# A hybrid attention block on one core: tiles at new address places, and one weight split ordered behind a product

## The chip, the core and the metric

The kernel runs on one core of a Trainium2 chip. The metric is device time in microseconds for one execution, and the time of a kernel is the median over its runs. The engines are named as the profile names them: PE is TensorE (matrix products), DVE is VectorE, ACT is ScalarE, POOL is GpSimd, and SP is SyncE, whose queue issues most of the DMA transfers.

## What is computed

One decoder block on 512 tokens of width 2048, in fp32. The normed input goes through one input projection. Half of the width feeds eight heads of sparse attention (width 128, two key groups: scores over compressed blocks, selected blocks and a window, mixed by gates); the other half feeds sixteen heads of sliding-window attention with sinks (width 64). Each head's result is multiplied by a SiLU of a gate projection, then comes the output projection, the residual and a final RMSNorm.

```python
h = _rmsnorm(x, norm_g[l])
proj = h @ w_in[l]
(qa, kca, vca, ksa, vsa, kwa, vwa, za, ga, qb, kb, vb, zb) = jnp.split(proj, offsets, axis=-1)
...
o_a = gates[..., 0:1] * o_cmp + gates[..., 1:2] * o_sel + gates[..., 2:3] * o_win
y_a = o_a.reshape(B, S, WIDTH_A) * jax.nn.silu(za)
...
y_b = o_b.reshape(B, S, WIDTH_B) * jax.nn.silu(zb)
x = x + jnp.concatenate([y_a, y_b], axis=-1) @ w_out[l]
return _rmsnorm(x, final_g)
```

## The kernel before

**Products.** Every fp32 operand is split into a high and a low word of the type fp32r: ACT copies (rounds) the high word, DVE subtracts it to get the low word (`split`, L541 to 544; `load_unit`, L88). `mm3` (L118 to 121) then issues three matmuls for one product: weights high with high, low with high, high with low. Most matmuls have 128x128 weights (the stationary operand) and 256 or 512 moving columns.

**Places.** A words tile is 1088 fp32 words long per partition, and 1024 of them are used. The argument of `words(place)` (L80) says at which word the used part begins: MOVING 0, EVEN 16, STILL 32, BELOW 48, so at 0, 64, 128 or 192 bytes into the tile. A word is 4 bytes, and the tile's length is a multiple of 256 bytes, so a place is the same modulo 256 bytes in every buffer of this kind. x's words `xh` and `xl` have tiles of their own (L108, L109), and later the heads' results `yh`, `yl` (L1001) are read back into the same memory for the output projection.

**Stages**, by the trace's clock: up to 45 us the sums for the norm and the first 512-column projections; 45 to 291 the sixteen sliding-window heads, interleaved with 512-column projections; 291 to 353 the compress stage, in which `tok_chunk` (x's words as weights, words of wv1 or wv0 moving) alternates with `compress_unit` (tokens' words as weights, words of cw1 moving); 353 to 425 keys and the first gated projections; 425 to 665 the eight sparse heads; 648 to 679 the last units of wo0 (the first part of the output projection); from 679 the rest of the output projection, built of products of summed blocks.

**Heads.** `pair(h)` (L669) makes one head's queries and gate by `seven(2 + h)` (L574), a scheme of seven block products named 22, p, 21, 12, u, w, q instead of eight, in which the weights are stationary (at STILL) and tokens' words move. `x1` to `x4` are the quarters of the weights, loaded by SP into the tiles `raw`, and `unit` (L546) splits them into whi and wlo. At the end of `pair` DVE multiplies the gate by the inverse root: `last["jj"]`, L677, printed as zr<-zr,rstdb; then ACT takes a tanh of it (L681, printed as st<-zr) and DVE finishes the SiLU (L682). The queries are rotated (POOL adds t<-t,t, L664) and split: qh on ACT (L260), ql on POOL (L261) for the heads 0 to 5. `attn_a` (L908) then does the scores (L932: sp<-KH,qh, sp<-KL,qh, sp<-KH,ql), the exponentials, transposes of the weights (tp) and the products with the values (op). `finish` (L270) multiplies op into the gated result st, which SP writes to memory as yd (L272). The heads 4 to 7 use the second key group, so KH and KL are loaded again (L1027) between head 3 and head 4.

**What sets the order.** Each engine works through its instructions in one order. The program's text gives dependencies, and a list planner places the instructions on the engines by them; `tc.issue_after(a)` adds the demand that what follows stands behind `a`. From about 426 us on this order changes wherever the dependencies or the buffers change.

## Time and profile before

| | us |
|---|---|
| median of three runs | 802.01 |
| the profiled execution's own time | 802.8 |
| its span, first to last instruction | 801.0 |
| PE busy | 789.6 (99%) |
| DVE busy | 686.3 (86%) |
| ACT busy | 504.7 (63%) |
| POOL busy | 108.3 (14%) |

Busy shares are averages over the whole span; how one stage is limited is read from the rows of that stage. In a timeline the first column is when an instruction starts, the second how long it takes; two matmuls overlap, so that the pace of PE is the difference between the starts of neighbours and not the duration. An idle time stands in brackets with what ended it.

### The profile page before, as it was taken

The page shows a single profiled execution, that of the slowest core. Times are in us where ns is not written, and L with a number is a line of the kernel's source. Part 1 is how long each engine was busy: PE and PEld are TensorE (multiplying, and loading weights), DVE is VectorE, ACT ScalarE, POOL GpSimd, SP SyncE. Part 2 cuts the span into 40 slices and gives each one's busy share as a digit, 9 for nine tenths or more (in the row PEclk, how much of TensorE's full clock was granted, in tenths as well). Part 3 has the DMA queues.
Part 4 walks back from the last instruction along what each step waited for, and adds up shares of the span by engine and source line. Part 5 has one row for each costly group of instructions (what it writes and reads, how often), then busy time and mean ns, then how long its engine had stood idle before and what let it go on. Part 6 is the DMA issues. An engine that isn't in the chain of part 4 may idle for free.

```text
span 801.0 us, 15316 instructions
## 1 busy us (share of the span) xinstructions
PE 789.6 (99%) x5693; PEld 739.1 (92%) x5693; DVE 686.3 (86%) x1407; ACT 504.7 (63%) x1103; POOL 108.3 (14%) x111
## 2 busy tenths in 40 slices
PE   9999999999999999999999999999999999999996
PEld 8788888888888899999999999999999999999996
DVE  7668988889989597759999999998999798978895
ACT  6646657655666356664447778777777867553545
POOL 3615002110121000323210110110100000000000
PEclk9999999999999999999999999999999999999998
DMA  7572243564373469887723213225216836797845
GB/s 239 172 242 81 79 144 106 171 171 150 101 210 106 158 200 281 257 269 194 207 82 106 68 53 119 82 92 159 71 50 216 296 120 219 257 266 193 258 86 211
DMA packets 49563, 131.05 MB, mean 164 GB/s; under 512 B 6000, under 2 KB 8848, under 8 KB 49488
## 3 DMA queue, kind: packets, MB, share of 16 engines
q1 hardware_dynamic: 43376, 110.89, 42.3%
q0 software_dynamic: 5824, 18.65, 10.5%
q8 instruction: 45, 0.74, 0.4%
q10 hardware_dynamic: 288, 0.52, 0.2%
q14 instruction: 30, 0.25, 0.1%
HBM read 113.23 MB, written 16.81 MB: 162 GB/s over the span
## 4 chain that ended last, share of the span: by engine, by line
PE 86%; DVE 6%; DMA 3%; ACT 2%; issue 2%; POOL 0%; SPq 0%; DVEq 0%; ACTq 0%
PE pj L119 16%; PE pj L121 15%; PE pj L120 15%; PE oa L120 5%; PE oa L119 5%; PE oa L121 5%; PE sp L932 4%; PE bank L121 2%; PE bank L120 2%; PE bank L119 2%; DMA xr<-xT 2%; DVE wlo L543 2%; PE tp L969 2%; PE tp L384 2%; DMA raw<-wq 1%
## 5 line engine op out<-in xcount | busy, mean ns | idle before, releaser
L119 PE MATMUL pj<-xh,whi 128*128 128x256 f32 (+1 forms) x592 | 196.9, 333 | 0.6 <-ACT t L608 0.5
L121 PE MATMUL pj<-xh,wlo 128*128 128x256 f32 (+1 forms) x592 | 196.2, 331 | 0.0
L120 PE MATMUL pj<-xl,whi 128*128 128x256 f32 (+1 forms) x592 | 196.1, 331 | 0.0
L119 PEld LDWEIGHTS pj<-xh,whi 128*128 128x128 f32 x592 | 111.4, 188 | 11.0 <-ACT t L608 0.9
L121 PEld LDWEIGHTS pj<-xh,wlo 128*128 128x128 f32 x592 | 111.4, 188 | 10.1
L120 PEld LDWEIGHTS pj<-xl,whi 128*128 128x128 f32 x592 | 111.4, 188 | 9.7
L543 DVE TENSOR_TENSOR wlo<-raw,whi 128x1024 fp32r<-128x1024 f32 (+2 forms) x80 | 92.9, 1172 | 7.8 <-ACT whi L542 7.2
L542 ACT ACTIVATE whi<-raw 128x1024 fp32r<-128x1024 f32 (+2 forms) x80 | 77.6, 985 | 30.7 <-DVE raw L581 11.5
L99 DVE TENSOR_TENSOR wlo<-raw,whi 128x1024 fp32r<-128x1024 f32 (+1 forms) x61 | 72.1, 1184 | 22.8 <-ACT whi L97 22.3
L97 ACT ACTIVATE whi<-raw 128x1024 fp32r<-128x1024 f32 (+1 forms) x60 | 56.6, 945 | 28.8 <-PE pj L120 14.8
L120 PE MATMUL oa<-wlo,xh 128*128 128x256 f32 x200 | 55.5, 278 | 0.0
L119 PE MATMUL oa<-whi,xh 128*128 128x256 f32 x200 | 55.4, 278 | 0.0
L121 PE MATMUL oa<-whi,xl 128*128 128x256 f32 x200 | 55.2, 276 | 0.0
L121 PE MATMUL pj<-pu,wlo 128*128 128x256 f32 x160 | 45.0, 281 | 0.5 <-DVE wlo L543 0.5
L119 PE MATMUL pj<-pu,whi 128*128 128x256 f32 x160 | 45.1, 282 | 0.4 <-DVE zr L581 0.4
L120 PE MATMUL pj<-pu,whi 128*128 128x256 f32 x160 | 44.7, 279 | 0.0
L289 DVE TENSOR_TENSOR pl<-tp,ph 128x512 fp32r<-128x512 f32 (+1 forms) x64 | 40.7, 651 | 3.1 <-ACT ph L288 2.9
L288 ACT ACTIVATE ph<-tp 128x512 fp32r<-128x512 f32 (+1 forms) x64 | 34.1, 560 | 9.6 <-PE tp L969 4.4
L363 ACT ACTIVATE ttb<-ttb,sums 128x256 f32<-128x256 f32 (+1 forms) x64 | 30.0, 471 | 14.4 <-DVE sums L356 14.4
L121 PEld LDWEIGHTS oa<-whi,xl 128*128 128x128 f32 x200 | 37.6, 188 | 0.0
L120 PEld LDWEIGHTS oa<-wlo,xh 128*128 128x128 f32 x200 | 37.6, 188 | 0.0
L119 PEld LDWEIGHTS oa<-whi,xh 128*128 128x128 f32 x200 | 37.5, 188 | 0.0
(401 smaller groups left out, 2369.8 us busy)
## 6 DMA issues: line engine op xcount, KB each, us to landing
raw<-wq SPq DMA_DIRECT2D x41, 512.0 KB, 4.4
raw<-wz SPq DMA_DIRECT2D x36, 512.0 KB, 4.0
cw<-cw SPq DMA_DIRECT2D x32, 256.0 KB, 4.0
raw<-wos SPq DMA_DIRECT2D x14, 512.0 KB, 5.9
rw<-wos SPq DMA_DIRECT2D x10, 512.0 KB, 4.8
xr<-xT SPq DMA_DIRECT2D x16, 256.0 KB, 3.4
rows<-xT SPq DMA_DIRECT2D x8, 512.0 KB, 4.7
raw<-wo SPq DMA_DIRECT2D x8, 512.0 KB, 6.0
```

The source lines that it names most:

```text
L97: last["hi"] = act.activation(hi[:, :width], rw[:, :width], AF.Copy).ins
L99: last["lo"] = dve.tensor_tensor(out=lo[:, :width], in0=rw[:, :width], in1=hi[:, :width].bitcast(F32), op=ALU.subtract).ins
L119: pe.matmul(ps, ah, bh, start=first, stop=False, skip_group_check=go_on)
L120: pe.matmul(ps, ah, bl, start=False, stop=False, skip_group_check=go_on)
L121: recent["mm"] = pe.matmul(ps, al, bh, start=False, stop=last, skip_group_check=go_on).ins
L288: act.activation(ph, tp, AF.Copy)
L289: dve.tensor_tensor(out=pl, in0=tp, in1=ph.bitcast(F32), op=ALU.subtract)
L363: act.activation(tv, tv, AF.Exp, bias=mn[:, e, v:v + 1], scale=-1.0, accum_out=dn[:, e, v:v + 1])
L384: pe.transpose(tp[:, o:o + P], tts[kt + s][:, v, c0:c0 + P], ident)
L542: split_hi = act.activation(hi, src, AF.Copy).ins
L543: last["lo"] = dve.tensor_tensor(out=lo, in0=src, in1=hi.bitcast(F32), op=ALU.subtract).ins
L932: pe.matmul(sp[:, a:b], qq[:, qs], kk[:, ko:ko + b - a], start=pi == 0, stop=pi == 2)
```

## The change

Most of it moves tiles. BELOW goes away: `compress_unit`'s words now begin at MOVING like those of `tok_chunk`. The words of wo0 and of the output projection's products (`halves`, `pair`) move from MOVING to EVEN, 64 bytes further. `yh` and `yl` begin 16 words (64 bytes) further in the memory of x's words, which are now one tile `slabs`; so a result that is read back can overlap two neighbouring rows of x's words. Small tiles get longer, `space` tiles are put in as pads, `vbf` takes a buffer of the tag `ob`, and the row flag moves from the tile gt to the tile small, with a small transfer of its own. The single matmul `step` ahead of the output projection gets other addresses. In the built program, counted modulo 256 bytes, a moving tile at MOVING starts at 128, at EVEN at 192, x's words at 192, and y's words at 192 before and 0 after.

One edit is about order: in head 1 (`seven(3)`, i == 3) the split of the quarter x3, which product 21 uses, is put behind `last["jj"]`, the multiply of head 0's gate by the inverse root.

```diff
 CMP = 32
-MOVING, EVEN, STILL, BELOW = 0, 16, 32, 48
+MOVING, EVEN, STILL = 0, 16, 32
 WARM = 40
...
     const = ctx.enter_context(sb("const"))
+    gt = const.tile([P, KT], F32, name="gt")
     wp = ctx.enter_context(sb("wp", bufs=3))
...
     bmask = tab[:, 512 + NQ * CMP:768 + NQ * CMP]
-    small = const.tile([P, 8], F32, name="small")
+    small = const.tile([P, 16], F32, name="small")
     rstd, eps = small[:, 0:NQ], small[:, NQ:NQ + 1]
...
     gates = const.tile([P, NQ, 24], F32, name="gates")
-    gt = const.tile([P, KT + 1], F32, name="gt")
-    rowvalid = gt[:, KT:KT + 1]
+    rowvalid = small[:, 8:9]
 
...
     xpool = ctx.enter_context(sb("xpool", side="right"))
-    xh = xpool.tile([P, KT, S], F32R, name="xh")
-    xl = xpool.tile([P, KT, S], F32R, name="xl")
+    slabs = xpool.tile([P, 2 * KT * S + 64], F32R, name="x")
+    xh, xl = [slabs[:, e * KT * S:(e + 1) * KT * S].rearrange("p (k s) -> p k s", s=S) for e in range(2)]
     angles = xstack.enter_context(sb("angles", side="right"))
...
 
-    flat = xh.rearrange("p k s -> p (k s)")
+    flat = slabs[:, 0:KT * S]
 
...
         if k == 0:
-            nc.sync.dma_start(gt, gT)
+            nc.sync.dma_start(gt, gT[:, 0:KT])
         nc.sync.dma_start(xr, xT[:, k, :])
...
         nc.sync.dma_start(tab, tabs)
+        nc.sync.dma_start(rowvalid, gT[:, KT:KT + 1])
     dve.tensor_tensor(out=cosB, in0=cosB, in1=rstdb, op=ALU.mult)
...
 
-    vbf = wb.tile([P, NQ, P], F32, name="vbf")
+    vbf = wb.tile([P, NQ, P], F32, name="vbf", tag="ob")
+    KBH = wb.tile([P, 2, S], F32R, name="KBH")
+    KBL = wb.tile([P, 2, S], F32R, name="KBL")
     sk = wb.tile([P, 5, 16], F32, name="sk")
...
     act.activation(sk[:, 1, :], sk[:, 0, :], AF.Copy, scale=-1.0)
-    KBH = wb.tile([P, 2, S], F32R, name="KBH")
-    KBL = wb.tile([P, 2, S], F32R, name="KBL")
     VB = wb.tile([P, NQ, 2, P], F32R, name="VB")
...
         for part in range(2):
-            sums = wk.tile([P, 3, 2, 2], F32, name="sums", tag="sums")
+            sums = wk.tile([P, 6, 2, 2], F32, name="sums", tag="sums")
             mn, dn, ex = sums[:, 0], sums[:, 1], sums[:, 2]
...
     VC = [kv.tile([P, P], F32R, name=f"VC{g}") for g in range(2)]
+    kv.tile([P, 48], F32, name="space")
     ahead = ExitStack()
...
         if not final:
-            u2 = unit(x3)
+            with tc.issue_after(last["jj"]) if i == 3 else nullcontext():
+                u2 = unit(x3)
             prod(pb[:, H0], u2, "21", False)
...
     early, ready = quarters[:1], quarters[1:]
-    places = [words(MOVING), words(BELOW), words(BELOW)]
+    places = [words(MOVING) for n in range(3)]
 
...
             cacc[1] = bank(4)
-        compress_unit(1, u, cacc[1], words(BELOW))
+        compress_unit(1, u, cacc[1], words(MOVING))
         if 1 <= u <= 3:
...
     KH, KL = [kv.tile([P, CMP + 1056], F32R, name=f"K{e}")[:, 0:CMP + 1024] for e in "HL"]
+    kv.tile([P, 16], F32, name="space")
     for e, k in enumerate((KH, KL)):
...
             tt = wa.tile([P, 1792 if pair else 768], F32, name=f"tt{pair}", tag=f"tt{pair}")
-            sums = wk.tile([P, 2, 2, 3], F32, name="sums", tag="sums")
+            sums = wk.tile([P, 4, 2, 3], F32, name="sums", tag="sums")
             mn, dn = sums[:, 0], sums[:, 1]
...
 
-    yh, yl = [[w[:, (2 * f + 1) % 17, :] for f in range(16)] for w in (xh, xl)]
+    yh, yl = [[slabs[:, (e * KT + (2 * f + 1) % 17) * S + 16:][:, 0:S] for f in range(16)] for e in range(2)]
 
...
                      (1, 3, (7,))):
-        hi, lo = load_unit(wo0[:, c, u], 1024, place=MOVING, loaded=first_units.pop(0) if first_units else None, after=last["qh"],
+        hi, lo = load_unit(wo0[:, c, u], 1024, place=EVEN, loaded=first_units.pop(0) if first_units else None, after=last["qh"],
                            after_lo=low_y[11] if (c, u) == (0, 2) else last["turn"])
...
                 combos(m)
+    cmb.tile([P, 48], F32, name="space3")
     banks1 = banks(1)
-    step(banks1[3], flat[:, 3 * S - 16:3 * S + 112], flat[:, 2 * S + 32:2 * S + 288])
+    step(banks1[3], flat[:, 2 * S:2 * S + P], flat[:, 3 * S - 16:3 * S + 240])
     for T in range(2):
...
     def halves(raw, to=None):
-        hi, lo = to or words(MOVING)
+        hi, lo = to or words(EVEN)
         split_to(hi, lo, raw)
...
             def pair():
-                return words(MOVING)
+                return words(EVEN)
 
...
                 act.activation(d[0], src, AF.Copy)

```

At the border from head 0 to head 1 the order moves on DVE. The numbers tell tiles of one name apart: t1_4493 is head 0's query and zr_4494 its gate, wlo_4984 is the low word of x3 for head 1's product 21, and raw_4922 the sum of two quarters. Before:

```order
L543 TENSOR_TENSOR wlo_4925<-raw_4922,whi_4924 128x1024
L662 TENSOR_TENSOR t1_4493<-t1_4493,cosA_115 128x512
L581 TENSOR_TENSOR zr_4494<-zr_4494,pj_4492 128x256
L543 TENSOR_TENSOR wlo_4984<-raw_4956,whi_4983 128x1024
L677 TENSOR_TENSOR zr_4494<-zr_4494,rstdb_68 128x512
L581 TENSOR_TENSOR raw_4922<-raw_4922,raw_4928 128x1024
L682 SCALAR_TENSOR_TENSOR st_4728<-st_4728,zr_4494 128x512
```

After (the same tiles have numbers 2 higher):

```order
L545 TENSOR_TENSOR wlo_4927<-raw_4924,whi_4926 128x1024
L665 TENSOR_TENSOR t1_4495<-t1_4495,cosA_114 128x512
L583 TENSOR_TENSOR zr_4496<-zr_4496,pj_4494 128x256
L680 TENSOR_TENSOR zr_4496<-zr_4496,rstdb_69 128x512
L583 TENSOR_TENSOR raw_4924<-raw_4924,raw_4930 128x1024
L545 TENSOR_TENSOR wlo_4986<-raw_4958,whi_4985 128x1024
L685 SCALAR_TENSOR_TENSOR st_4730<-st_4730,zr_4496 128x512
```

The split of x3 now stands behind both the multiply by rstdb and the sum of the quarters. On ACT, at the same place, the query's high word qh, the tanh st<-zr and the copy of head 1's product 22 (t1_4914<-pj) stand before as

```order
L542 ACTIVATE whi_4983<-raw_4956 128x1024
L260 ACTIVATE qh_4694<-t1_4493 128x512
L681 ACTIVATE st_4728<-zr_4494 128x512
L608 ACTIVATE t1_4914<-pj_4912 128x256
L542 ACTIVATE whi_5013<-raw_4922 128x1024
```

and after as

```order
L544 ACTIVATE whi_4985<-raw_4958 128x1024
L684 ACTIVATE st_4730<-zr_4496 128x512
L261 ACTIVATE qh_4696<-t1_4495 128x512
L610 ACTIVATE t1_4916<-pj_4914 128x256
L544 ACTIVATE whi_5015<-raw_4924 128x1024
```

The tanh has gone ahead of qh. PE's order at this border is the same in both. On SP, where the keys of the second group are loaded again, the issues before are (yd10 is the result of head 2)

```order
L1027 DMA KL_4242<-Kd_73 128x1056
L1027 DMA KH_4241<-Kd_73 128x1056
L272 DMA yd10_86<-st_5542 128x512
L563 DMA raw_6919<-wq 128x1024
L1030 DMA VH_2836<-Vd_74 128x256
L1030 DMA VL_2837<-Vd_74 128x256
```

and after

```order
L1031 DMA KL_4243<-Kd_73 128x1056
L273 DMA yd10_86<-st_5544 128x512
L1031 DMA KH_4242<-Kd_73 128x1056
L565 DMA raw_6921<-wq 128x1024
L565 DMA raw_6927<-wq 128x1024
L565 DMA raw_6933<-wq 128x1024
L565 DMA raw_6961<-wq 128x1024
```

KH has moved behind the write of head 2's result, and the first values stand behind four loads of weights instead of one.

## Rows read from the trace of the kernel before

**Rows 1.** The page, part 1: busy us, share of the span, instructions
```profile
PE 789.6 (99%) x5693; PEld 739.1 (92%) x5693; DVE 686.3 (86%) x1407; ACT 504.7 (63%) x1103; POOL 108.3 (14%) x111
```

**Rows 2.** Stretches, PE alone: from:to, length, busy (matmuls), granted clock, DMA, GB/s
```profile
291.00:353.00 62.00, 62.00 (x513) 1.00 0.88 270
353.00:425.00 72.00, 70.44 (x602) 1.00 0.56 155
425.00:648.00 223.00, 222.79 (x1871) 1.00 0.38 125
...
679.00:793.00 114.00, 114.00 (x1006) 1.00 0.74 214
```

**Rows 3.** Timeline, PE, compress stage: start, duration, line, out<-moving,weights; columns; count
```profile
299.83 0.28 PE L120 MATMUL bank<-wlo,xh 128*128 128x256 f32 x1
...
302.89 0.28 PE L119 MATMUL bank<-whi,xh 128*128 128x256 f32 x1
...
303.84 0.28 PE L708 MATMUL pj<-whi,F 128*128 128x256 f32 x1
...
305.32 0.28 PE L709 MATMUL pj<-wlo,F 128*128 128x256 f32 x1
```

**Rows 4.** Timeline, PE, output projection
```profile
700.00 0.28 PE L120 MATMUL oa<-wlo,uh 128*128 128x256 f32 x1
...
702.94 0.28 PE L119 MATMUL oa<-whi,xh 128*128 128x256 f32 x1
```

**Rows 5.** Timeline, PE, heads
```profile
531.34 0.28 PE L119 MATMUL pj<-xh,whi 128*128 128x256 f32 x1
...
532.51 0.28 PE L977 MATMUL op<-ph,VL 128*128 128x256 f32 x1
...
553.70 0.28 PE L119 MATMUL pj<-xh,whi 128*128 128x256 f32 x1
...
555.52 0.28 PE L120 MATMUL pj<-xl,whi 128*128 128x256 f32 x1
```

**Rows 6.** Timeline, PE, border of head 0 and head 1
```profile
420.85 0.29 PE L932 MATMUL sp<-KH,ql 128*128 128x288 f32 x1
421.66 0.39 PE L119 MATMUL pj<-xh,whi 128*128 128x256 f32 x1 [0.52 <-ACT t L608]
```

**Rows 7.** Timeline, ACT, same border
```profile
420.71 0.63 ACT L681 ACTIVATE st<-zr 128x512 f32<-128x512 f32 x1 [2.15 <-DVE zr L677]
421.25 0.36 ACT L608 ACTIVATE t<-pj 128x256 f32<-128x256 f32 x1
```

**Rows 8.** Timeline, DVE, same border
```profile
415.77 0.69 DVE L662 TENSOR_TENSOR t<-t,cosA 128x512 f32<-128x512 f32 x1
416.37 0.42 DVE L581 TENSOR_TENSOR zr<-zr,pj 128x256 f32<-128x256 f32 x1
416.70 2.27 DVE L543 TENSOR_TENSOR wlo<-raw,whi 128x1024 fp32r<-128x1024 f32 x1
418.90 1.78 DVE L677 TENSOR_TENSOR zr<-zr,rstdb 128x512 f32<-128x512 f32 x1
420.60 1.21 DVE L581 TENSOR_TENSOR raw<-raw 128x1024 f32<-128x1024 f32 x1
```

**Rows 9.** Timeline, POOL, same border
```profile
416.61 1.28 POOL L664 TENSOR_TENSOR t<-t,t 128x512 f32<-128x512 f32 x1 [21.54 <-DVE t L662]
418.64 1.49 POOL L261 TENSOR_TENSOR ql<-t,qh 128x512 fp32r<-128x512 f32 x1 [0.75 <-ACT qh L260]
```

**Rows 10.** Timelines of PE, DVE and SP around the finish of head 2
```profile
525.12 0.61 PE L992 MATMUL op<-pd,VF 128*128 128x128 f32 x4
...
528.62 0.68 DVE L270 SCALAR_TENSOR_TENSOR st<-op,st 128x512 f32<-128x512 f32 x1
...
529.34 0.32 SPq L272 DMA_DIRECT2D yd<-st  x1
```

**Rows 11.** DMA issues, 500 to 560: tile, count, KB, median us to landing
```profile
KH<-Kd SPq DMA_DIRECT2D x1, 528.0 KB, 4.4
```

## Prediction

> **What bounds the kernel now.** I read first the busy shares of the page: TensorE is busy for 99% of the span [rows 1], so time can only go where TensorE waits or where its instructions stand further apart than they must. The busy time of TensorE by stretch says that waiting is small: 222.79 of 223 us in the eight heads, 114.00 of 114 us in the output projection, at a granted clock of 1.00 in each [rows 2]. That is the upper of the two levels, 2.4 GHz, so no clock is to be won back. What is left is the distance between starts, so the third view is TensorE's timeline, read by its first column. All rows chosen there are the same work, 128x128 weights and 256 moving columns, yet there are two paces. In the compress stage 26 steps from 299.83 to 302.89 take 3.06 us, 117.7 ns each; the next products, of compress_unit, take 113.8 ns over 13 steps from 303.84 to 305.32 [rows 3]. In the output projection 26 steps take 2.94 us, 113.1 ns each [rows 4]. In the heads both occur: 117.0 ns over ten steps from 531.34, 113.8 over sixteen from 553.70 [rows 5]. Take 113.1 and 117.7: **a long step costs 4.6 ns more than a short one**.
>
> Where does the pace change? Compare with the addresses in the built program, modulo 256 bytes. A words tile at MOVING starts at 128, EVEN at 192, STILL at 0, BELOW at 64; x's words at 192. In the output projection every moving operand starts at 128 and the pace never changes. In the compress stage tok_chunk moves words at 128 and compress_unit moves words at 64, and the pace flips at that border [rows 3]. Transposes and fp32 matmuls can also leave either pace behind them. Of all pairs of neighbouring fp32r matmuls, 188 differ by 64 bytes (either sign) in the moving operand before the change, and 11 after; steps of 64 in the stationary operand alone remain.
>
> Taking each distance between two starts, I count as long the 256-column matmuls with 115.5 to 125 ns to the next: 211 of 314 in the compress stage, 701 of 1442 in the heads, 5 of 1003 in the output projection. Each stretch is a row of [rows 2], which also counts transposes, narrower and wider matmuls.
>
> **The change, part by part.**
>
> *Compress stage.* compress_unit's words move from 64 to 128, the place of tok_chunk's. What remains between them is a step in the weights alone. The first of four tok_chunk runs ends at the short pace in the trace, the next three (48 matmuls each) are at the long one, and so are about 45 of the compress_unit matmuls. If the pace now stays as the first run leaves it, 144 + 45 steps turn from long to short: 189 x 4.6 = 0.87 us; of the other long steps some stand behind small fp32 products and stay. I take **-0.8**, bounds -1.0 (all 211) and +0.5 (the 103 others turn long).
>
> *Sliding-window heads.* Here projections of 512 columns are interleaved with scores and 256-column products at other places; 77 of the 188 steps lie here. All distances above the short pace (113.1 per 256 columns) sum to 2.2 us in this stage. Transposes also reset the pace, so I take a fifth: **-0.4**, bounds 0 and -2.2.
>
> *NSA heads and wo0's units.* The edit moves wo0's words, pair and halves from MOVING to EVEN and shifts y's words by 64 bytes, so wo0's products have the same places as the heads' products between which they stand. 72 of the 188 steps lie in 425 to 648. But each head also has transposes, after which either pace was seen. Between 353 and 425, where there are two steps of 64 and few transposes, 161 of 562 are long (29%). If the heads go from 49% long to about a third, 1442 x 0.16 x 4.6 ns = 1.06 us. I take **-1.1**, bounds 0 and -3.2 (all 701).
>
> *Output projection.* From 128 to 192 for moving and 192 to 0 for weights, all alike before and after: 0. Pads, the row flag's transfer and vbf's shared buffer add no compute instruction: 0, covered by TensorE's work in the opening.
>
> *Head 1's split behind head 0's product.* TensorE waits once here: after the third score matmul at 420.85 product 21 starts only at 421.66 [rows 6], 0.69 us later than the step of 0.12 would have it. Its releaser is ACT's copy of product 22 at 421.25, queued behind the tanh at 420.71 [rows 7], which waits for VectorE's zr<-zr,rstdb, 418.90 to 420.68; that stood behind the split wlo, 416.70 to 418.97 [rows 8]. Both were stretched: the multiply takes 0.69 in the row at 415.77 for the same shape, and it ended just after POOL's ql did (420.13); the split ended 1.08 us after POOL's sum of 416.61 to 417.89 [rows 9]. Order after: zr sum, multiply, sum of raws, split. The multiply begins at 416.8, is held until 417.9 and ends at about 418.5; the sum of raws (1.21, [rows 8]) ends at 419.7; the split, as long as that sum, ends at 420.9. On ACT tanh runs 418.5 to 419.15, the high word qh, a pass of the same size as the tanh, to 419.75, the copy to 420.1. So the old wait goes. But POOL's ql, ready to start at 419.75, now meets the split, begun at 419.7, and would run from 420.9 for 1.28 to 1.49 us [rows 9], to 422.2; the third score matmul, due at 420.85, needs it. That is a new wait of 1.2 to 1.4 in place of 0.69: +0.6. If ql comes first the split ends at 422.4 and the third matmul of product 21, due at 421.2, waits as long. Bounds: -0.7 (no collision) and +1.2. I take **+0.4**, nearer to the collision because the margin is 0.05 us.
>
> The Trainium skill, "SBUF — State Buffer", section "Who interferes with whom", says that a VectorE instruction with two SBUF inputs and a GpSimd instruction that reads SBUF exclude each other for the whole instruction. By that rule the collision happens and the sum is +0.6; by the unstretched durations alone it would be -0.7. The trace agrees with the page: 1.78 us against 0.69 for one shape [rows 8].
>
> *The heads' order.* A list order decides VectorE, ACT, SP and TensorE from 426 us on, and it comes out differently. Before, TensorE waits 0.21 us in all in that stretch [rows 2]; I cost it at 0, hidden by the products of the next head that lie between, and treat the tightest place as a rival.
>
> Sum: -0.8 - 0.4 - 1.1 + 0.4 = -1.9. The profiled execution is 802.8, so 800.9; the median of the runs is 802.0, 0.8 less, and on that scale the forecast is **800.1**.
>
> **Rivals.**
>
> 1. *The pace stays short nearly everywhere.* For it: the output projection, where all places are alike, has 5 long steps in 1003. Against it: there are no transposes there. It would give 211 + 701 + 161 = 1073 x 4.6 = 4.9 us, and 2.2 in the sliding-window heads: 802.0 - 7.1 + 0.4 = 795.3.
>
> 2. *Only the compress stage gains,* since transposes reset the pace to chance everywhere else: 802.0 - 0.8 + 0.4 = 801.6. For it: from 425 to 620 each stretch of 40 to 55 us has 41% to 66% long, whatever was interleaved in it.
>
> 3. *Places do nothing.* The flips could come from which bank is written, which changes at the same borders. Then only the split counts: 802.4. Of operand addresses the Trainium skill, "SBUF — State Buffer", section "Specifications (TRN2)", knows lines of 16 bytes, on whose borders all these places lie; by that alone places would change nothing. The trace disagrees so far: two paces for one shape [rows 3].
>
> 4. *Slower: the reload of head 4's keys.* KH's transfer now stands on SP behind yd (the result of head 2), and that waits for VectorE's finish. Before, product op ended with four matmuls from 525.12 (0.61), the finish came at 528.62, yd's issue at 529.34 [rows 10]; KH takes 4.4 us from issue to landing [rows 11]. After, 66 matmuls stand between that product and the first score on the new keys, about 8.0 us at 0.12. With the finish 3.5 us late as before and 0.7 for itself, 0.3 for yd and 4.4 for KH are 8.9: 0.9 late. In the new order fewer instructions stand ahead of the finish (one sum of 1.2), so 6.6 and no wait. If two splits' time more (2.4) comes in, 11.3: 3.3 late, 802.0 - 1.9 + 3.3 = 803.4. It decides against the change from a finish that starts 4.5 us after the product.
>
> **How the numbers follow.** Forecast (gain of 1 to 4): 0.52, its own range 798.3 to 801.2. Rival 1: 0.12. Rival 2: 0.15. Rival 3: 0.08. Rival 4 or another new wait in the heads: 0.13. The range 796.5 to 804.0 takes in rivals 2, 3, most of 4, and part of 1. A difference of 2%, 16 us, about what a measurement of this kernel can tell from no change, is beyond every case: all long steps together are worth 7.1. So faster 0.01, same 0.97, slower 0.02.
>
> **What would show it.** Right: in the compress stage of the changed kernel all tok_chunk and compress_unit steps at 113 to 114 ns; in the heads a third long; between 415 and 424 no wait for ACT's t, but one for ql or for the split of 0.5 to 1.3 us. Wrong: alternating paces as before (rival 3), or a wait on DMA KH at head 4's first score (rival 4). What would upset the sum is a wait on another transfer in 426 to 665, where the order is new.

## The result

| | kernel before | changed kernel |
|---|---|---|
| median (us) | 802.76 of 6 runs | 810.76 of 6 runs |
| profiled execution, its span | 802.8, 801.0 | 806.0, 804.2 |
| PE busy | 789.6 | 792.2 |
| DVE busy | 686.3 | 681.3 |

The ratio is 1.0085, with an interval of 1.0065 to 1.0104: the change makes the kernel 0.65% to 1.04% longer, where 800.1 was forecast in a range of 796.5 to 804.0. One of the six runs of the kernel before took 909.72 us, and the ratio is formed without it. The executions of the changed kernel lie wide: 806.0, 807.7, and four from 810.3 to 812.6. The first profile is of the 806.0, so it holds the smaller part of the loss; a second profile, of an execution of 810.94, comes with the first experiment below.

PE alone by stretch, as in [rows 2], in the changed kernel's first profile:

```profile
291.00:353.00 62.00, 62.00 (x520) 1.00 0.87 273
353.00:425.00 72.00, 70.94 (x602) 1.00 0.54 151
425.00:648.00 223.00, 221.43 (x1845) 1.00 0.37 124
...
679.00:793.00 114.00, 113.79 (x999) 1.00 0.71 205
```

The granted clock is 1.00 as before. In the compress stage 520 matmuls lie where 513 did: that part gained. In the heads 1845 lie where 1871 did, and PE is idle 1.57 us where it was 0.21. The waits of PE from 425 to 665, first in the changed kernel (line waited for: us, times, longest):

```profile
PE pj L121 <- DVE wlo L545: 1.2, 2, 0.8
PE sp L936 <- DVE sums L942: 0.4, 2, 0.2
```

and in the kernel before:

```profile
PE sp L932 <- DVE sums L938: 0.2, 1, 0.2
```

The rows that answer to those of the border, on PE [rows 6], ACT [rows 7], DVE [rows 8] and POOL [rows 9], in that order:

```profile
420.24 0.40 PE L936 MATMUL sp<-KH,ql 128*128 128x288 f32 x1 [0.45 <-POOL ql L262]
420.66 0.38 PE L119 MATMUL pj<-x,whi 128*128 128x256 f32 x1
```

```profile
416.80 0.63 ACT L684 ACTIVATE st<-zr 128x512 f32<-128x512 f32 x1 [1.95 <-DVE zr L680]
417.34 0.62 ACT L261 ACTIVATE qh<-t 128x512 fp32r<-128x512 f32 x1
```

```profile
415.15 1.62 DVE L680 TENSOR_TENSOR zr<-zr,rstdb 128x512 f32<-128x512 f32 x1
416.69 1.21 DVE L583 TENSOR_TENSOR raw<-raw 128x1024 f32<-128x1024 f32 x1
417.83 1.21 DVE L545 TENSOR_TENSOR wlo<-raw,whi 128x1024 fp32r<-128x1024 f32 x1
418.96 1.77 DVE L685 SCALAR_TENSOR_TENSOR st<-st,zr 128x512 f32<-128x512 f32 x1
```

```profile
418.04 2.15 POOL L262 TENSOR_TENSOR ql<-t,qh 128x512 fp32r<-128x512 f32 x1 [1.81 <-ACT qh L261]
```

The wait for ACT's t is gone, and the third score matmul waits for ql instead, which ran from 418.04 to 420.19 because the split of x3 (417.83 to 419.04) was ahead of it. That much came as forecast.

Two sums serve below, both taken over the distances between neighbouring starts of PE's matmuls. **Pace**: what the distances of fp32r matmuls have above 113.3 ns per 256 columns, as far as it is under 40 ns. **Waits**: what they have above it where that is over 130 ns. Before, they are 9.3 and 3.8 us for the whole span; in the first profile of the changed kernel 10.8 and 6.0. These two differences, 1.5 and 2.1 before rounding, are a little more than the 3.2 us by which the spans differ; all other distances, most of them at transposes, give 0.3 back.

### The profile page after: what moved, and what is told of

It is laid out like the page before. It is cut to its first block, busy times and chain, and to the rows that moved or that the text cites. A ratio compares the mean times of both kernels' runs of the same rounds, so it can differ in the third digit from the quotient of the medians.

```text
span 804.2 us, 15336 instructions
## 1 busy us (share of the span) xinstructions
PE 792.2 (99%) x5693; PEld 741.5 (92%) x5693; DVE 681.3 (85%) x1407; ACT 504.4 (63%) x1103; POOL 107.6 (13%) x111
## 4 chain that ended last, share of the span: by engine, by line
PE 84%; DVE 8%; issue 3%; ACT 2%; DMA 2%; POOL 0%; POOLq 0%; ACTq 0%; DVEq 0%
PE pj L121 15%; PE pj L119 15%; PE pj L120 15%; PE oa L120 4%; PE oa L121 4%; PE oa L119 4%; PE bank L119 3%; PE bank L120 3%; PE sp L936 3%; PE bank L121 3%; DVE wlo L545 2%; DMA raw<-wq 2%; PE tp L385 2%; PE tp L973 1%; PE spb L350 1%
## 5 line engine op out<-in xcount | busy, mean ns | idle before, releaser
L119 PE MATMUL pj<-x,whi 128*128 128x256 f32 (+1 forms) x592 | 197.0, 333 | 0.3 <-DVE t L583 0.2
L121 PE MATMUL pj<-x,wlo 128*128 128x256 f32 (+1 forms) x592 | 196.4, 332 | 0.8 <-DVE wlo L545 0.8
L120 PE MATMUL pj<-x,whi 128*128 128x256 f32 (+1 forms) x592 | 196.2, 331 | 0.0
L121 PEld LDWEIGHTS pj<-x,wlo 128*128 128x128 f32 x592 | 111.4, 188 | 11.1 <-DVE wlo L545 1.0
L119 PEld LDWEIGHTS pj<-x,whi 128*128 128x128 f32 x592 | 111.4, 188 | 10.7 <-issue 0.4
L120 PEld LDWEIGHTS pj<-x,whi 128*128 128x128 f32 x592 | 111.6, 189 | 9.7
L120 PE MATMUL oa<-wlo,x 128*128 128x256 f32 x200 | 55.7, 278 | 0.0
L121 PE MATMUL oa<-whi,x 128*128 128x256 f32 x200 | 55.6, 278 | 0.0
L119 PE MATMUL oa<-whi,x 128*128 128x256 f32 x200 | 55.6, 278 | 0.0
L119 PEld LDWEIGHTS oa<-whi,x 128*128 128x128 f32 x200 | 37.7, 188 | 0.0
L120 PEld LDWEIGHTS oa<-wlo,x 128*128 128x128 f32 x200 | 37.6, 188 | 0.1
L121 PEld LDWEIGHTS oa<-whi,x 128*128 128x128 f32 x200 | 37.6, 188 | 0.0
```

Source lines behind the costliest of these rows:

```text
L119: pe.matmul(ps, ah, bh, start=first, stop=False, skip_group_check=go_on)
L120: pe.matmul(ps, ah, bl, start=False, stop=False, skip_group_check=go_on)
L121: recent["mm"] = pe.matmul(ps, al, bh, start=False, stop=last, skip_group_check=go_on).ins
```

## The experiments

Each is compared with executions of the kernel before on the same chip, so the ratio counts; the profile's own numbers are of one execution. The sums are over the whole span: all 3.8 us of waits before lie ahead of 425 us, and this early part differs from execution to execution.

| kernel | median us | ratio, interval | pace, waits in its profile |
|---|---|---|---|
| changed kernel again | 810.78 | 1.0099 (1.0086 to 1.0112) | 13.4, 8.0 |
| before, split behind the product | 810.38 | 1.0090 (1.0065 to 1.0114) | 10.3, 6.2 |
| changed, without the split's edit | 804.54 | 1.0017 (1.0007 to 1.0026) | 11.2, 3.5 |
| changed, old output places | 809.97 | 1.0086 (1.0073 to 1.0099) | 13.2, 8.8 |
| changed, two more step matmuls | 808.59 | 1.0076 (1.0057 to 1.0094) | 11.6, 6.9 |
| before, late split at 685 us | 808.31 | 1.0073 (1.0049 to 1.0098) | 9.9, 6.7 |
| without the edit, one step more | 804.21 | 1.0023 (1.0009 to 1.0036) | 10.0, 4.6 |
| before, compress places | 804.65 | 1.0014 (1.0001 to 1.0027) | 10.3, 5.1 |
| before, words at EVEN at the end | 808.70 | 1.0067 (1.0047 to 1.0087) | 16.2, 1.8 |
| changed, early split at 685 us | 807.07 | 1.0047 (1.0027 to 1.0067) | 10.2, 7.9 |
| changed, early split and a step | 808.19 | 1.0052 (1.0038 to 1.0066) | 9.9, 7.0 |

**The changed kernel again.** No edit.

> The changed kernel again, unaltered. Its profiled execution was 806.0 us, 3.2 above the one of before (2.1 in waits of TensorE, 1.5 in the pace, -0.3 elsewhere), but four of its six executions lie at 810.3 to 812.6. Theory P (pace): in those the stretch from 667 us to the end, about 1100 matmuls with no wait in it, runs at the long pace; a profile of such an execution shows 117.7 ns from start to start at 700 us and 4 to 5 us more between 680 us and the end, and the same waits as before. Theory W (waits): the longer executions have longer waits of TensorE between 426 and 665 us, 4 to 5 us more in their sum, and 113.3 ns at 700 us. Executions: 806 to 813 by both.

Its profile is of 810.94 us. The pace in the output projection: first this execution, then the one of 806.0, each with the first and last matmul of a stretch of 28 and 29.

```profile
699.73 0.28 PE L119 MATMUL oa<-whi,uh 128*128 128x256 f32 x1
...
702.91 0.28 PE L119 MATMUL oa<-whi,uh 128*128 128x256 f32 x1
```

```profile
699.75 0.28 PE L119 MATMUL oa<-whi,uh 128*128 128x256 f32 x1
...
702.92 0.28 PE L120 MATMUL oa<-wlo,uh 128*128 128x256 f32 x1
```

27 steps in 3.18 us are 117.8 ns; 28 steps in 3.17 us are 113.2, as in [rows 4]. From 679 us on the pace sums to 4.5 us in the longer execution and 0.2 in the shorter: 4.3 of the 5.0 us between their spans. Elsewhere the longer one has 1.7 less in pace and 2.1 more in waits (0.7 in the heads, 0.4 at the border, the rest before 400 us). So theory P holds, and the small waits, too, differ from execution to execution. The clock is no rival: it is 0.997 to 0.999 in the long and the short executions alike. Where the two profiles part can be seen: both have the same wait, first the execution of 810.94:

```profile
685.23 0.28 PE L119 MATMUL oa<-whi,x 128*128 128x256 f32 x1
685.73 0.38 PE L120 MATMUL oa<-wlo,ph 128*128 128x256 f32 x1 [0.22 <-DVE wlo L1056]
```

```profile
684.25 0.28 PE L119 MATMUL oa<-whi,x 128*128 128x256 f32 x1
684.74 0.39 PE L120 MATMUL oa<-wlo,ph 128*128 128x256 f32 x1 [0.21 <-DVE wlo L1056]
```

Up to that wait both are at the short pace. Behind it the one is long for all the matmuls that follow; the other takes four long steps and is short. So a wait draws the pace anew, short or long, and a stream with neither transposes nor steps of 64 in its moving operand keeps what it drew. The waits in the heads show it as well. Behind those near 513, 574 and 603 us the pace settles long in the profile of 806.0 and short in that of 810.94; behind the one near 597 us it is the other way round. The kernel before has no wait at 685 us.

**The two halves apart.** The split's edit on the kernel before:

```diff
         if not final:
-            u2 = unit(x3)
+            with tc.issue_after(last["jj"]) if i == 3 else nullcontext():
+                u2 = unit(x3)
```

> The kernel before with the split of head 1's x3 behind the product with the inverse root, and nothing else: its order on every engine is that of the changed kernel, its places are those of before. Theory O (the new order costs, by its waits of TensorE after 426 us: 1.8 in 580 to 620, 0.7 in two score waits, and 0.2 at head 1's border): 804 to 805, executions within 2 us of each other. Theory A (the places cost, the order does not): 801 to 803. The prediction's term for this edit was +0.4: 802.4 with a wait for POOL's ql of 0.4 to 1.3 at 420 us in place of the wait for ACT's t.

And the changed kernel without that edit:

```diff
         if not final:
-            with tc.issue_after(last["jj"]) if i == 3 else nullcontext():
-                u2 = unit(x3)
+            u2 = unit(x3)
```

> The changed kernel without the edit of the split: its order on every engine is that of before (but for the row flag's transfer and the one merged opening transfer), its places are the new ones. Theory O: 800 to 802, no waits of TensorE between 426 and 665 us beyond 0.3. Theory A with pace P: 804 to 809, spread over 4 us or more, and the excess lies in the pace. The prediction's term for the places was -2.3: 799.7.

The two are a clean division. The first has, instruction for instruction, the order of the changed kernel on every engine, and the second that of the kernel before; only the row flag's small transfer goes with the places. The edit alone costs +0.9%, the places alone +0.17%. So the whole new order comes from one edit, and nearly the whole loss from the new order; the places, which were to bring 2.3 us, cost 1.4. Theory O gave 804 to 805 for the first and missed the draw at 685 us: the profile, of the shortest execution (806.07), has waits of 6.2 us and a short end, while the others go to 814.5. For the second theory O was too low (800 to 802), and theory A had the level but expected a spread of 4 us where it is 2.9.

In the second, the pace sum of the compress stage is 1.96, no less than before (1.90), though the places are those of the changed kernel, where it is 1.2. Its timeline shows why:

```profile
296.79 0.28 PE L120 MATMUL bank<-wlo,x 128*128 128x256 f32 x1
...
299.39 0.28 PE L711 MATMUL pj<-wlo,F 128*128 128x256 f32 x1
299.51 0.39 PE L119 MATMUL bank<-whi,x 128*128 128x256 f32 x2
299.76 0.38 PE L120 MATMUL bank<-wlo,x 128*128 128x256 f32 x1
...
300.10 0.28 PE L119 MATMUL bank<-whi,x 128*128 128x256 f32 x1
...
303.99 0.28 PE L120 MATMUL bank<-wlo,x 128*128 128x256 f32 x1
```

Up to 299.39 the steps are 113 ns (23 in 2.60 us); at 299.51 the next two products start 0.1 us late; from 300.10 on they are 117.9 (33 in 3.89 us), and stay so for the 190 matmuls up to the end of this part. The same small wait stands in the profile of the changed kernel, and there the draw was short.

**Old places for the output projection.** wo0's words, halves and pair at MOVING, y's words without the 16 words' shift, the old step matmul.

```diff
-    yh, yl = [[slabs[:, (e * KT + (2 * f + 1) % 17) * S + 16:][:, 0:S] for f in range(16)] for e in range(2)]
+    yh, yl = [[slabs[:, (e * KT + (2 * f + 1) % 17) * S:][:, 0:S] for f in range(16)] for e in range(2)]
...
-        hi, lo = to or words(EVEN)
+        hi, lo = to or words(MOVING)
```

> The changed kernel with the places of wo0 and of the output projection as before: words at MOVING, y's words without the shift of 16 words, the old step matmul. Order on every engine as in the changed kernel. Theory P: the stretch from 667 us runs short as before in every execution: 804.5 to 806.5, spread under 2 us. If the longer executions have their excess elsewhere (theory W, or the pace in the compress stage or the heads): 806 to 813 as the changed kernel.

809.97: theory P's 804.5 to 806.5 was wrong for this kernel, and for a reason of its own. The pads of the change had moved the tile of the first product's weights, so these were at 0 with the moving words at 128: of the first 25 steps four in five are long even before the wait at 688 us, and behind it the stream is long too, up to about 702 us (pace from 679 us on: 3.2). From there on, too, part of its products have their operands 128 bytes apart: 266 of 335 such matmuls are long, and 154 of 456 of those at 64 bytes. It shows that the places of the two operands must fit each other, and decides nothing about the draw.

**Step matmuls behind the waits.** Two more, into a bank whose contents are overwritten:

```diff
             product(bb, u22, "22", True)
+            if n == 1:
+                step(banks1[3], yh[2][:, 48:176], u22[1][0][:, 48:304])
...
             product(ba, u12, "12", False)
+            if n == 1:
+                step(banks1[3], yh[2][:, 48:176], u12[1][0][:, 48:304])
```

The lines left out give the words of the two products the names u22 and u12; the products stay as they were.

> The changed kernel with two more step matmuls (their results are not used) in the output projection: one behind the first two products (96 matmuls), one behind the third. In every trace so far the pace is short some five matmuls after a step matmul. Theory P (a wait of 0.2 to 0.9 us at 685 us draws the pace anew, and without transposes or steps of 64 the stream keeps it to the end, 4.5 us if long): the output projection is at 113.4 ns behind the second of the two in every execution; executions lie at 805.5 to 807.5 instead of 809 to 813. Theory C (the longer executions come from something else that makes the pace long at the end, a clock or memory state): executions as the changed kernel's, 809 to 813, and the pace is long again soon behind the step matmuls.

Five of six executions lie within 0.33 us (808.47 to 808.80), where the changed kernel's spread over 6.6. In the profile the wait at 685 drew the long pace, the first step matmul ended it 70 matmuls later, and to the end the pace is short: 0.6 us from 679 on. So the step matmul does end a long draw. The level is 1 us above what was expected; in its profile the compress stage drew long (2.0 instead of 1.2), which makes up 0.8 of it, but that the other executions did so too is not shown.

**The wait put into the kernel before.** One idle DVE instruction behind the split of the output projection's first weights, and a demand that keeps the first and the second product in one order:

```diff
         u3 = [halves(load(raw(), 0, g)) for g in range(2)]
+        if n == 1:
+            late_word = u3[1][1][:, 0:256].bitcast(F32)
+            dve.tensor_tensor(out=u3[1][1][:, 0:256], in0=late_word, in1=late_word, op=ALU.max)
...
-            product(bb, [halves(r) for r in r22], "22", True)
+            u22 = [halves(r) for r in r22]
+            with tc.issue_after(recent["mm"]) if n == 1 else nullcontext():
+                product(bb, u22, "22", True)
```

> The kernel before with one idle VectorE instruction of 0.42 us (a maximum of a quarter of the low word with itself) behind the split of the second half of the output projection's first weights, so that its 26th matmul has to wait some 0.2 to 0.4 us; the first and second product are kept in one order. Nothing before 665 us differs. Theory P: the wait draws the pace anew; part of the executions, or all, lie 4 to 5 us higher (807 to 809), the others at 802.5 to 804, and where the profile is of a long one it shows 117.7 ns from 685 us on. Rival (the wait costs only itself): all executions at 802.5 to 804, pace 113.4.

The planner put the instruction further back than meant, and the wait became 3.2 us instead of 0.2 to 0.4:

```profile
684.38 0.38 PE L120 MATMUL oa<-wlo,ph 128*128 128x256 f32 x1 [3.22 <-DVE wlo L1270]
```

The profiled execution, 806.07, is the shortest and is short behind this wait: 802.6 and 3.5 for the wait. The five others lie 1.7 to 5.7 us higher. A draw, whose long side is 4.5, is one reason they could have; the granted clock is another. Over the execution it is 0.997 in the profiled one and 0.993 to 0.995 in these five, while in all other kernels here, the kernel before included, it is 0.997 to 0.999. An estimate from these shares: 0.002 of 806 us are 1.6 us, 0.004 are 3.2. So for 807.79, 807.82 (both 0.995) and 808.81 (0.993) the clock is enough; for 810.05 (0.994) about 1.6 us is left, and for 811.77 (0.995) about 4.1, which is near a long draw. There is no profile of a longer execution, so this kernel does not show that a wait put into the kernel before makes its end long.

**A step matmul in the compress stage**, on the changed kernel without the split's edit:

```diff
+        if u == 0:
+            step(vacc[0][0], xh[:, 0, 0:P], places[1][0][:, 48:304])
```

> The changed kernel without the edit of the split (order of before, 804.5) and with one more step matmul in the compress stage, behind the first two compress_unit products. In the profile of the kernel without it a wait of 0.1 us in those products left the pace long for the 190 matmuls up to the end of wv1, 0.8 us. Theory P: those are at the short pace now; the excess of the stage falls from 1.96 to about 1.2 us, median 803.5 to 804. If the places do not hold the pace: 804.5, excess of the stage about 1.9.

The stage's pace sum fell from 1.96 to 1.18, as expected: the places do let the stage keep a pace, and the step matmul made it the short one. The median is 0.3 us lower, the ratio no better (1.0023 against 1.0017, intervals overlapping): 0.8 us in one stage is near what this comparison can resolve.

**The compress stage alone**, on the kernel before:

```diff
-    places = [words(MOVING), words(BELOW), words(BELOW)]
+    places = [words(MOVING) for n in range(3)]
...
-        compress_unit(1, u, cacc[1], words(BELOW))
+        compress_unit(1, u, cacc[1], words(MOVING))
```

with the same step matmul.

> The kernel before with the compress stage's places of the change (compress_unit's words at MOVING) and one step matmul behind the first two compress_unit products; all else as before. Theory P (equal places let the stream keep its pace, and the step matmul makes it the short one): the stage's excess over 113.3 ns falls from 1.9 to 1.2 us, and nothing else changes: 0.5 to 0.9 us below the kernel before. If the places hold nothing: 1.9 and no gain. The prediction's term for this part alone was -0.8.

A miss: 1.0014, and the stage's pace sum rose to 2.2. The reason is in the addresses: in the kernel before, the weights of compress_unit (the tile F) start at 128 modulo 256, and only the change's pads move them to 192. With the words moved alone, moving operand and weights start at the same place, and nearly every one of those matmuls is long, and the tok_chunk products between them too; the step matmul among them did not help.

**The distance between the two operands** was then tried by itself, on the kernel before:

```diff
     def halves(raw, to=None):
-        hi, lo = to or words(MOVING)
+        hi, lo = to or words(EVEN)
...
             def pair():
-                return words(MOVING)
+                return words(EVEN)
```

> The kernel before with only the output projection's moving words (halves, pair) at EVEN: 192 modulo 256 bytes, as the weights there (y's words), where both were 64 apart before. Order as before. Theory D (what counts is the distance between the places of moving operand and weights): the pace in the output projection is another one for all its 1007 matmuls, 117 to 118 ns, 4 to 5 us more: 806.5 to 808. Theory S (only steps between neighbours count): no step, pace short: 802 to 804.

Theory D holds: +0.67%, 808.7, a little above its range of 806.5 to 808. In the profile

```profile
699.72 0.28 PE L120 MATMUL oa<-wlo,uh 128*128 128x256 f32 x1
...
702.96 0.28 PE L120 MATMUL oa<-wlo,xh 128*128 128x256 f32 x1
```

27 steps in 3.24 us, 120 ns. Of the 992 matmuls from 679 us to 801 only two groups of 24, whose words still start 64 bytes below the weights, are short. The order is as before, and behind 425 us there is no new wait.

**The wait at 685 us taken away** in the changed kernel, by letting DVE do the sums of blocks after the split:

```diff
+        lo_u3 = last["lo"]
...
-                dve.tensor_tensor(out=ch[g], in0=ch[g], in1=other, op=ALU.add)
+                with tc.issue_after(lo_u3):
+                    dve.tensor_tensor(out=ch[g], in0=ch[g], in1=other, op=ALU.add)
```

> The changed kernel with the sums of blocks for product 12 behind the split of the output projection's first weights on VectorE, so that the split is ready 1.2 us earlier and the 26th matmul need not wait. The heads, with their waits, are as in the changed kernel. Theory P: without the wait at 685 us the pace stays short after the step matmul in every execution: 806 to 808.5 with a spread of 1 to 2 us, and 113.4 ns to the end. If the longer executions of the changed kernel have another cause: 809 to 813.

807.07, in theory P's range and 3.7 us under the changed kernel (a ratio of 1.0047 against 1.0099), for moving 1.2 us of DVE work; PE's order is the same but for one matmul. The wait is gone from the profile and the end is short (0.2 us from 679 on). A smaller wait of 0.37 at 694.83 is left, so a draw is left too, and the executions still spread over 3.1 us. With a step matmul behind that one as well:

> The changed kernel with both: the sums of blocks behind the split (as in the kernel without the wait at 685 us) and a step matmul behind the third product of the output projection, where that kernel still had a wait of 0.4 us (695 us). Theory P: no wait is left behind the step matmul, so no draw; about 113.4 ns to the end in every execution, 806 to 807.5, and the spread is under that of the kernel with the sums alone (806.2 to 809.3). What remains above the kernel before (802.8) is then the waits in the heads and at head 1's border (3 us) and the pace ahead of 680 us (0 to 2 us). If the spread stays 3 us, other stretches carry it.

The end is short in its profile (0.2). Against executions of 804.36 for the kernel before on this chip it is 1.0052, the same as without the step, and the spread, 2.6, is hardly smaller; expected was less than that of the kernel ahead. A further small wait is seen there in the distances, at about 713 us. No version beat the kernel before.

## Why the prediction was wrong

**The limit** was named rightly: PE, by waits and by pace, at a clock that does not change. The price of a long step, 4.6 ns, held: 117.8 against 113.2 over the last thousand matmuls, 4.5 us.

**The failed step: the heads' order, costed at 0.** The text saw that the order comes out differently from 426 us on, and looked for what a transfer could do there; "another new wait in the heads" had a share of a chance of 0.13 and no length of its own. What it did not ask is what a new order on DVE, which is 86% busy, does to the splits that PE reads. PE's rows in the changed kernel; before, there was one wait of 0.21 for sums and none for a split:

```profile
513.53 0.60 PE L936 MATMUL sp<-KH,qh 128*128 128x288 f32 x2 [0.18 <-DVE sums L942]
...
573.66 0.60 PE L936 MATMUL sp<-KH,qh 128*128 128x288 f32 x2 [0.18 <-DVE sums L942]
...
597.55 0.38 PE L121 MATMUL pj<-x,wlo 128*128 128x256 f32 x1 [0.76 <-DVE wlo L545]
...
602.66 0.39 PE L121 MATMUL pj<-pu,wlo 128*128 128x256 f32 x1 [0.45 <-DVE wlo L545]
```

and DVE at the largest:

```profile
595.26 0.17 DVE L954 TENSOR_SCALAR sums<-sums 128x6 f32<-128x6 f32 x1
...
595.68 0.42 DVE L583 TENSOR_TENSOR t<-t,pj 128x256 f32<-128x256 f32 x1
...
596.27 1.23 DVE L545 TENSOR_TENSOR wlo<-raw,whi 128x1024 fp32r<-128x1024 f32 x1
```

The split starts at 596.27, behind a run of DVE work without a gap, and ends just as PE goes on. In the kernel before the same split (wlo_7387 there, wlo_7389 here) was ready 1.9 us before PE read it:

```profile
597.44 1.21 DVE L543 TENSOR_TENSOR wlo<-raw,whi 128x1024 fp32r<-128x1024 f32 x1
```

```profile
600.58 0.28 PE L121 MATMUL pj<-xh,wlo 128*128 128x256 f32 x1
```

As sums over distances the waits in the heads are 2.5 us in one profile and 3.1 in the other; in the kernel before this sum is 0, as its one wait of 0.21 stands behind a transpose. The 3.1 are a good third of the 8.2 us between the spans of the longer execution and of the kernel before.

**The larger part is a mechanism that the text had in its hands and did not use.** It said that transposes can leave either pace, and priced each wait as its own length. But a wait draws the pace too, so a wait costs its length and what the stream behind it does until something else sets the pace. In the heads that is up to about 60 matmuls; at 685 us it is about a thousand. The split that is 0.21 us late there was 0.40 us early before, right behind the sum of blocks:

```profile
679.00 1.22 DVE L1287 TENSOR_TENSOR ch<-ch,raw 128x1024 f32<-128x1024 f32 x1
680.13 1.22 DVE L1052 TENSOR_TENSOR wlo<-raw,whi 128x1024 fp32r<-128x1024 f32 x1
```

```profile
681.75 0.28 PE L120 MATMUL oa<-wlo,ph 128*128 128x256 f32 x1
```

In the new order two operations of 0.41 us stand between the two:

```profile
681.67 1.22 DVE L1292 TENSOR_TENSOR ch<-ch,raw 128x1024 f32<-128x1024 f32 x1
682.80 0.41 DVE L1074 TENSOR_TENSOR yp<-yp 128x256 f32<-128x256 f32 x1
683.14 0.41 DVE L1056 TENSOR_TENSOR x<-yp,x 128x256 fp32r<-128x256 f32 x1
683.48 1.21 DVE L1056 TENSOR_TENSOR wlo<-raw,whi 128x1024 fp32r<-128x1024 f32 x1
```

The late split costs 4.5 us in the profiled long execution. By their times eight of ten executions of the changed kernel lie where that one does; only this one of them was profiled. For the profile of 810.94, whose span is 8.2 us longer than before, the sum is: 4.5 pace at the end, 3.1 waits in the heads, 0.7 at the border, 0.4 at 685, and -0.5 for everything else.

**The border** (term +0.4): right in mechanism and size. The wait went from ACT's t to POOL's ql; from 0.69 us over the pace to 0.91 in one profile and 1.35 in the other, so +0.2 to +0.7. The Trainium skill, "SBUF — State Buffer", section "Who interferes with whom", has the rule that two such instructions exclude each other. The trace agrees with it: ql took 2.15 us with the split and the finish of SiLU beside it, and POOL's two rows before took 1.28 and 1.49 [rows 9]. The working came to +0.6 by that rule.

**The compress stage** (term -0.8): -0.7 in five profiles of the new places, +0.1 in two; right as the value of a short draw, wrong as a certainty. (The kernel with a step matmul in this stage is not among the seven.) A loss was within the bounds, at most +0.5, but it had no chance of its own.

**The sliding-window heads** (term -0.4): wrong in sign. From 141 to 291 us the pace sum is 1.7 in all profiles with the new places and 1.4 to 1.5 in all with the old ones: +0.25.

**NSA heads and wo0's units** (term -1.1): wrong. With the order of before and the new places the sum from 425 to 679 is 5.0, before it was 4.2. From 620 to 679 us alone it goes from 0.5 to 1.4 and again to 1.4 with the step matmul in the compress stage: a run of 49 and one of 66 matmuls behind the same scores and transposes are long where they were short. So there the pace behind transposes was no matter of chance but repeats with the places, and the new ones repeat the worse side. The new order does the same without them: the kernel before with the split's edit alone, at the old places, has 1.3 there, as the changed kernel has, so in the changed kernel the two are not to be added. The prediction's sign, a third of the heads' matmuls long, did not come: by its count 847 and 621 are long in the two profiles, where 701 were. Counting steps of 64 (188 down to 11) counted events and not the time behind each.

**Rival 4** (head 4's keys): did not happen, and by little. The finish of head 2, the issue, and the first score on the new keys:

```profile
529.93 0.61 PE L996 MATMUL op<-pd,VF 128*128 128x128 f32 x4
...
538.25 0.29 PE L936 MATMUL sp<-KH,qh 128*128 128x288 f32 x1
```

```profile
530.60 0.68 DVE L271 SCALAR_TENSOR_TENSOR st<-op,st 128x512 f32<-128x512 f32 x1
```

```profile
532.04 0.36 SPq L1031 DMA_DIRECT2D KH<-Kd  x1
```

```profile
KH<-Kd SPq DMA_DIRECT2D x1, 528.0 KB, 5.2
```

532.04 + 5.2 = 537.2, 1.0 us ahead of the score, against 1.4 in the working (8.0 less 6.6; 4.4 was used for a transfer that took 5.2).

**Rival 3** (places do nothing) is refuted by the kernel with the words at EVEN: one shape, one order, 120 ns for 113.2. The Trainium skill, "SBUF — State Buffer", section "Specifications (TRN2)", knows lines of 16 bytes, on whose borders all these places lie; the measurement differs from what that alone would make of it, and decides.

What stays open: why a draw falls long or short; why the kernel with two step matmuls lies 1 us above its sum; and what the longer executions of the kernel with the late split hold, clock or pace.

## What to carry to other kernels

An edit to one instruction's dependency can reorder everything behind it when a planner makes the order, and it then has to be priced by the new order's tightest deliveries on the busiest helper engine, not by the edit. Making all neighbours alike removes what disturbs a stream and also what would put it right: ask what the last event ahead of a long uniform stretch is, and whether it leaves a good state every time. If a kernel's executions spread more after a change, profile a long one before explaining the median.

## What the hardware showed that was not expected

A wait of 0.1 to 0.9 us can change the pace of every matmul behind it (113.2 or 117.8 ns for 256 columns) for as long as the stream stays uniform, here for a thousand matmuls, and the same wait falls either way from execution to execution: at 685 us and at four waits in the heads the two profiles of one program drew opposite paces. A single extra matmul whose moving operand starts 64 bytes lower was followed by the short pace within five matmuls in every trace in which moving operand and weights otherwise kept 64 bytes distance; behind products with equal places it did not help. With both operands at the same place modulo 256 bytes nearly all matmuls were long: 120 ns.
